# Landing the first weight tiles in idle activation tiles, and moving casts behind the q/k result

## The chip, the cores and the metric

The kernel runs on one core of a Trainium2 chip. The metric is the device time of one execution in microseconds; less is better.

## The reference

One decoder layer on 256 tokens of width 1024, in float32:

```python
z = h @ w_in[l]                                   # 1024 -> 512 (u) + 512 (q) + 512 (k) + 512 (v)
pool_out = multiscale_pool(u, w_pool, pool_scale) # trailing-window means, per-group linear
attn_out = moba_attention(q, k, v)                # 8 heads of 64; at 256 tokens plain causal attention
mix = concat([pool_out, attn_out]) @ w_out
h = layer_norm(ALPHA * h + mix)
h = layer_norm(ALPHA * h + memory_cross_attention(h, mem, w_xq, w_xkv, w_xo))   # 4 heads of 256
h = layer_norm(ALPHA * h + swiglu(h, w_gate, w_up, w_down))                     # inner width 2816
```

## The kernel before

Every large product is made from three float32r products (`three`, and the same by hand in `product_qk`): an operand is split into a high part, which ACT casts (L79 for weights, L280 for activations), and a low part, which DVE subtracts (L80, L281). So each weight tile w0, w1, ... that is loaded from HBM costs one ACT cast and one DVE subtraction before PE can use it. The order of the instructions on each engine is the order of the program text; no scheduler changes it.

`Stream` holds the list of all weight tiles in order of use. `fetch` issues loads, on SP's queue unless told otherwise; a load takes one of `RAW_BUFS` = 4 raw tiles, so the load of tile n goes out when tile n-4 has been cast and subtracted. `prepare` casts and subtracts the next tiles, running first what `before` has noted for a tile (loads of x, of the memory, of the norm weights). `get` hands a tile to a product; unless `held` is set it also prepares one more tile, up to `AHEAD` = 6 tiles past those used. With `held` and `loads` set it only issues loads. Weight tiles here are 256 KB for w0 to w5 (half a 128-row block of the q and k columns) and 512 KB from w6 on (a whole block, or half of a 1 MB piece).

The stretch that the change touches, in order:

- `keep_busy(BUSY)` gives PE 16 transposes of the identity, whose result nobody reads, while the first loads are under way. They wait for the identity that POOL makes.
- x arrives transposed in four steps (`load_xt`, into `xr`) and is split into `xT` (`split_xt`). The steps from block 4 on are noted with `before`, so their loads are issued when the cast of the weight tile of that block is due.
- `product_qk(k)` for the eight blocks k of 128 rows adds q and k, transposed, into four PSUM banks `pqk0` to `pqk3`: 24 matmuls of 256 columns per block. w0 to w10 hold its weights. In the last block `keep_qk` empties each bank into `qkT` as soon as it is complete, two on ACT (L311, L315) and two on DVE (L313, L317).
- From k = 6 on `held` and `loads` are set: no casts ahead, only loads. After the loop both are cleared.
- The `fac` factors of the pooling are made on DVE (L356, L357).
- The v product (`pv`, w11 to w14) takes two of the four banks that the q/k result has left; between its pieces stand `scores(0, 0)` and `scores(0, 1)` (masked scores, their maximum, exponentials on ACT, scaling on DVE). Then `probs_t(0)`, `probs_t(1)` transpose the probabilities into PSUM and copy them out to `sb` (one copy on DVE, one on ACT), between pieces of the u product (w15 to w18); `attend(0)` (L424) multiplies them with v into a bank `po` of the pool of four that the scores and the transposes use as well.
- w19 to w26 are for the memory's keys. `split_mem` splits the memory (`mr`, loaded in one piece of 1 MB) into `mT`. `load_x` loads the tokens `xt`, also 1 MB, right behind the load of w20.

The pool `acts` has nine tiles of 128 x 2048 float32 (tag `a8`), for `xt`, `xT`, `mT`, `xr`, `qkT`, `cT` and later tiles in turn.

Of the kernel before, what the change touches and what calls it, by code (L numbers as in the profile page):

```python
# [8 lines left out]
F32 = mybir.dt.float32  # L9
# [5 lines left out]
P = 128  # L15
# [16 lines left out]
RAW_BUFS, W_BUFS, AHEAD = 4, 8, 6  # L32
A8_BUFS = 9
PR_BUFS = 6
BUSY = 16


def r32(t):
# [3 lines left out]
class Stream:  # L42


    def __init__(self, nc, pool):
        self.nc, self.pool = nc, pool
        self.src, self.raws, self.tiles, self.notes = [], [], [], {}
        self.used, self.held, self.loads = 0, True, False

    def add(self, src, parts=2):  # L50

        n = src.shape[1] // parts
        first = len(self.src)
        self.src += [src[:, i * n:(i + 1) * n, :] for i in range(parts)]
        return range(first, len(self.src))
# [4 lines left out]
    def fetch(self, upto, queue):  # L60

        while len(self.raws) < upto:
            src = self.src[len(self.raws)]
            raw = self.pool.tile(list(src.shape), F32, tag="raw", name=f"w{len(self.raws)}r", bufs=RAW_BUFS)
            queue.dma_start(raw, src)
            self.raws.append(raw)

# [38 lines left out]
def decoder_layer(  # L106
# [3 lines left out]
    nc = tc.nc  # L110
    cp = ctx.enter_context(tc.tile_pool(name="const", bufs=1))
    wp = ctx.enter_context(tc.tile_pool(name="weights", bufs=W_BUFS))
    ap = ctx.enter_context(tc.tile_pool(name="acts", bufs=A8_BUFS))
# [5 lines left out]
    def a8(name, dt=F32):  # L119
        return ap.tile([P, KD, S], dt, tag="a8", name=name)  # L120

    def bank(name):
        return pb.tile([P, 512], F32, tag="b", name=name)
# [5 lines left out]
    ws = Stream(nc, wp)  # L129
# [5 lines left out]
    def rows(w, k0, c0, nk=2, width=D):  # L135
        return ws.add(w[k0 * P:(k0 + nk) * P, c0:c0 + width].rearrange("(k p) n -> p k n", p=P))

    c_qk = [ws.add(w_in[k * P:(k + 1) * P, 512:1536].rearrange("p (j n) -> p j n", j=2), 2 if k < 3 else 1)
            for k in range(KD)]
# [16 lines left out]
        nc.sync.dma_start(xt, x.rearrange("(t p) d -> p t d", p=P))  # L156

    xr = a8("xr")

    def load_xt(k, n=2):  # L160
        nc.sync.dma_start(xr[:, k:k + n, :], x_t[:, k:k + n, :])

    def split_xt(k, n=2):
        split(xT[0][:, k:k + n, :], xT[1][:, k:k + n, :], xr[:, k:k + n, :])
# [35 lines left out]
    ident = cp.tile([P, P], F32, name="ident")  # L200
# [78 lines left out]
    def split(h, l, ps):  # L279
        nc.scalar.copy(h, ps)  # L280
        nc.vector.tensor_sub(l, ps, r32(h))  # L281
# [17 lines left out]
    def keep_busy(n):  # L299

        ps = bank("busy")
        for _ in range(n):
            nc.tensor.transpose(ps[:, :P], ident, ident)

    qk = [accbank(f"pqk{i}").rearrange("p (f t) -> p f t", f=2) for i in range(4)]

# [12 lines left out]
    def product_qk(k):  # L319

        x_hi, x_lo = pair(xT, ALL, k)
        for j in range(2):
            hi, lo = ws.get(c_qk[k], j)
            for part in (((hi, x_hi), (hi, x_lo)), ((lo, x_hi),)):
                for i in (2 * j, 2 * j + 1):
                    for f in range(2):
                        c = 2 * (i % 2) + f
                        for n, (w, y) in enumerate(part):
                            nc.tensor.matmul(qk[i][:, f, :], w[:, c * P:(c + 1) * P], y,
                                             start=k == 0 and f == 0 and n == 0 and w is hi,  # L330
                                             stop=k == KD - 1 and w is lo, skip_group_check=True)
                    if k == KD - 1 and w is lo:
                        keep_qk(i)
            ws.done(c_qk[k], j)

    keep_busy(BUSY)
    for k in range(2, KD, 2):
        if k > 2:
            ws.before(c_qk[k][0], lambda k=k: load_xt(k))
        ws.before(c_qk[k][0], lambda k=k: split_xt(k))  # L340
    load_xt(0, 1)
    ws.fetch(1, nc.scalar)
# [1 line left out]
    load_xt(1, 1)  # L344
    ws.fetch(4, nc.sync)
    load_xt(2)
    split_xt(0, 1)
    ws.prepare(2)
    split_xt(1, 1)
    ws.held = False  # L350
    for k in range(KD):
        ws.held = ws.loads = k >= 6
        product_qk(k)
    ws.held = ws.loads = False
    for g, w in enumerate(WINDOWS):
# [450 lines left out]
```

## Time and profile before

| | |
|---|---|
| median of three timed runs | 391.63 us (390.73 to 391.84) |
| the profiled execution, whole | 393.3 us |
| its span, first to last instruction | 391.3 us |
| PE busy | 378.2 us |
| DVE busy | 246.1 us |
| ACT busy | 175.7 us |
| moved by DMA | 71.91 MB |

The profiled execution is one execution: every duration below comes from it. In the lists in order of time a row has the start and the length in us, the engine, the line of the kernel, the operation, what is written and read, and in brackets how long the engine stood idle before it and what ended that. A DMA row "SPq" is the issue on SP's queue; the landing is a separate figure. Tiles are named as in the program: w16r is the raw load of weight tile 16, w16h its high part, w16l its low part.

### The profile page before, as it was taken

To read this page: it belongs to the slowest core of one execution; us is meant where nothing else is said; L and a number is where in the kernel's file an instruction comes from. 1 tells how busy PE (TensorE), PEld (TensorE's weight loads), DVE (VectorE), ACT (ScalarE), POOL (GpSimd) and SP (SyncE) were. 2 spreads that over 40 slices of the span, in tenths; PEclk is the share of its full clock that TensorE was granted. 3 is DMA by queue.
4 is the path that set the end of the run, shared out by engine and by line. 5 is a ranking of instruction groups with operands and counts; after the bars stand their busy time and mean duration, and the time that the engine had idled before them with its cause. 6 is when DMAs were issued, how large, how long until landed. Compare 5 with 4: busy or idle time off the path is not lost.

```text
span 391.3 us, 5454 instructions
## 1 busy us (share of the span) xinstructions
PE 378.2 (97%) x2118; PEld 327.4 (84%) x2118; DVE 246.1 (63%) x340; ACT 175.7 (45%) x262; POOL 28.8 (7%) x35
## 2 busy tenths in 40 slices
PE   8998999999999999999999999999999999999982
PEld 8995879898888899998878888888888888888872
DVE  4467898776288775656887664557546456554274
ACT  5355766564332645545336553335446245344000
POOL 1000004700420000000500000000000000000000
PEclk9999999999999999999999999999999999999997
DMA  7879753845715884334507846663654964852011
GB/s 214 306 220 339 252 203 90 340 162 175 257 54 142 275 295 150 108 109 160 163 0 268 272 160 214 210 216 122 203 191 143 309 214 138 296 172 101 0 54 54
DMA packets 21689, 71.91 MB, mean 184 GB/s; under 512 B 2464, under 2 KB 3232, under 8 KB 21536
## 3 DMA queue, kind: packets, MB, share of 16 engines
q1 hardware_dynamic: 21232, 71.05, 55.0%
q10 hardware_dynamic: 432, 0.52, 0.4%
q8 instruction: 16, 0.26, 0.3%
q14 instruction: 9, 0.07, 0.1%
HBM read 70.52 MB, written 1.05 MB: 183 GB/s over the span
## 4 chain that ended last, share of the span: by engine, by line
PE 79%; DVE 7%; DMA 6%; ACT 4%; POOL 2%; issue 1%; SPq 0%; POOLq 0%; ACTq 0%; DVEq 0%
PE pg L223 10%; PE pg L221 10%; PE pg L222 10%; PE acc L221 7%; PE acc L223 7%; PE acc L222 7%; DMA w9r<-in_w_in 2%; PE pxk L221 2%; PE pxq L223 2%; PE pxq L221 2%; PE pxq L222 2%; PE pxk L222 2%; PE pxk L223 2%; PE xv L223 2%; PE xv L221 2%; PE xv L222 2%
## 5 line engine op out<-in xcount | busy, mean ns | idle before, releaser
L710 DVE TENSOR_TENSOR sg<-sg,pg 128x256 f32<-128x256 f32 x22 | 9.2, 420 | 34.9 <-ACT sg L709 34.9
L709 ACT ACTIVATE sg<-pg 128x256 f32<-128x256 f32 x22 | 8.4, 383 | 47.0 <-PE pg L223 46.8
L544 POOL TENSOR_TENSOR rs<-rs,mhalf 128x1 f32<-128x1 f32 x6 | 5.7, 955 | 199.2 <-DVE rs L543 199.2
L533 DVE SCALAR_TENSOR_TENSOR r<-h,acc 128x256 f32<-128x256 f32 (+1 forms) x12 | 6.0, 501 | 13.0 <-PE acc L223 13.0
L281 DVE TENSOR_TENSOR gTl<-pgt,gTh 128x512 fp32r<-128x512 f32 x11 | 7.1, 686 | 9.7 <-ACT gTh L280 9.7
L363 ACT ACTIVATE pr<-pr,mx 128x128 f32<-128x128 f32 (+1 forms) x16 | 7.2, 448 | 12.0 <-DVE mx L374 11.8
L280 ACT CAST gTh<-pgt 128x512 fp32r<-128x512 f32 x11 | 6.0, 589 | 14.4 <-PE pgt L716 14.4
L363 ACT ACTIVATE xpr<-xs,mx 128x256 f32<-128x256 f32 x8 | 3.7, 470 | 12.4 <-DVE mx L374 12.4
L536 DVE BATCH_NORM_STATS2 st<-r 128x6 f32<-128x512 f32 (+1 forms) x16 | 9.0, 560 | 0.5
L548 DVE SCALAR_TENSOR_TENSOR r<-r,mv,g 128x512 f32<-128x512 f32 (+1 forms) x14 | 9.2, 668 | 0.0
L436 POOL TENSOR_TENSOR win<-upad 128x271 f32<-128x271 f32 x4 | 3.6, 891 | 61.6 <-DVE pr L370 61.6
L280 ACT CAST h2Th<-tp 128x512 fp32r<-128x512 f32 x4 | 2.4, 588 | 11.8 <-PE tp L291 11.8
L80 POOL TENSOR_TENSOR w61l<-w61r,w61h 128x1024 fp32r<-128x1024 f32 x1 | 2.4, 2442 | 69.9 <-ACT w61h L79 69.9
L553 DVE SCALAR_TENSOR_TENSOR h<-r,rs,b 128x512 f32<-128x512 f32 x8 | 6.0, 752 | 1.9 <-POOL rs L544 1.8
L436 POOL TENSOR_TENSOR win<-win 128x269 f32<-128x269 f32 (+2 forms) x6 | 6.7, 1118 | 0.5
L533 DVE SCALAR_TENSOR_TENSOR r<-xt,acc 128x512 f32<-128x512 f32 x4 | 2.7, 681 | 6.0 <-PE acc L223 6.0
L716 PEld LDWEIGHTS pgt<-ident,sg 128*128 128x128 f32 x44 | 5.2, 140 | 0.8
L716 PE MATMUL pgt<-ident,sg 128*128 128x128 f32 x44 | 5.8, 272 | 0.0
L368 DVE RECIPROCAL sm<-sm 128x2 f32<-128x2 f32 x12 | 2.0, 164 | 5.9 <-ACT xpr L363 4.5
L281 DVE TENSOR_TENSOR xTl<-xr,xTh 128x512 fp32r<-128x512 f32 (+1 forms) x5 | 2.9, 582 | 4.3 <-ACT xTh L280 4.2
L374 DVE TENSOR_REDUCE mx<-xs 128x2 f32<-128x512 f32 x4 | 2.8, 692 | 4.4 <-PE xs L223 4.4
L291 PEld LDWEIGHTS tp<-ident,h 128*128 128x128 f32 x32 | 3.8, 140 | 2.0 <-issue 0.7
(1085 smaller groups left out, 1428.8 us busy)
## 6 DMA issues: line engine op xcount, KB each, us to landing
g<-in_ln_g SPq DMA_DIRECT2D x3, 512.0 KB, 7.1
b<-in_ln_b SPq DMA_DIRECT2D x3, 512.0 KB, 8.0
mr<-in_mem_t SPq DMA_DIRECT2D x1, 1024.0 KB, 7.3
xt<-in_x SPq DMA_DIRECT2D x1, 1024.0 KB, 7.8
xr<-in_x_t SPq DMA_DIRECT2D x3, 256.0 KB, 5.6
w6r<-in_w_in SPq DMA_DIRECT2D x1, 512.0 KB, 4.8
w7r<-in_w_in SPq DMA_DIRECT2D x1, 512.0 KB, 6.9
w8r<-in_w_in SPq DMA_DIRECT2D x1, 512.0 KB, 8.6
```

What stands on the lines that cost most here:

```text
L221: nc.tensor.matmul(ps, wa, ya, start=start, stop=False, skip_group_check=part)
L222: nc.tensor.matmul(ps, wa, yb, start=False, stop=False, skip_group_check=part)
L223: nc.tensor.matmul(ps, wb, ya, start=False, stop=stop, skip_group_check=part)
L280: nc.scalar.copy(h, ps)
L281: nc.vector.tensor_sub(l, ps, r32(h))
L363: nc.scalar.activation(dst[:, j, :], src[:, j, :], AF.Exp, bias=mx[:, j:j + 1], scale=1.0, accum_out=sm[:, j:j + 1])
L436: nc.gpsimd.tensor_add(nxt[:, 2 * n - 1:], cur[:, 2 * n - 1:], cur[:, n - 1:PADW + S - n])
L533: nc.vector.scalar_tensor_tensor(self.r[:, s], self.tok[:, s], ALPHA, acc, op0=OP.mult, op1=OP.add)
L536: nc.vector.bn_stats(self.st[:, self.n, :], self.r[:, c0:c1])
L548: nc.vector.scalar_tensor_tensor(self.r[:, s], self.r[:, s], self.mv[:, 0:1], gb[self.i][0][:, s], op0=OP.subtract, op1=OP.mult)
L710: nc.vector.tensor_mul(sg, sg, ps[:, CW:])
L716: nc.tensor.transpose(pt[:, f, t * P:(t + 1) * P], sgs[c][:, t, f * P:(f + 1) * P], ident)
```

## The change

The first seven weight tiles no longer take raw tiles: `homes` gives each of them a part of one of two `a8` tiles. The loads of w4 to w10 and of all of x are issued in one go before the first cast, instead of one by one as raw tiles come free and as casts fall due. From w7 on the raw tiles are used as before, so w7 to w10 have the four of them from the start and w11 waits for w7's.

`held` and `loads` are set from block 5 on instead of 6. In the built program that moves the casts of w12 and w13 from before `keep_qk` to behind it on ACT and DVE, those of w14 and w15 from before `scores(0, 0)` to behind it, and that of w16 from before `scores(0, 1)` to behind it. The order of SP's loads stays the same.

`keep_busy` gives PE nine plain products of a tile of zeros (`spark`, set by DVE), instead of sixteen transposes of the identity.

```diff
-BUSY = 16
+BUSY = 9
...
+        self.homes = {}
...
         while len(self.raws) < upto:
             src = self.src[len(self.raws)]
-            raw = self.pool.tile(list(src.shape), F32, tag="raw", name=f"w{len(self.raws)}r", bufs=RAW_BUFS)
+            raw = self.homes.pop(len(self.raws), None)
+            if raw is None:
+                raw = self.pool.tile(list(src.shape), F32, tag="raw", name=f"w{len(self.raws)}r", bufs=RAW_BUFS)
             queue.dma_start(raw, src)
...
     xr = a8("xr")
+    for i in range(2):
+        home = ap.tile([P, 4, 512], F32, tag="a8", name=f"w0to{3 + 3 * i}")
+        if i == 0:
+            ws.homes.update({n: home[:, n:n + 1, :] for n in range(4)})
+        else:
+            ws.homes.update({4: home[:, 0:1, :], 5: home[:, 1:2, :], 6: home[:, 2:4, :]})
...
         ps = bank("busy")
+        spark = cp.tile([P, P], F32, name="spark")
+        nc.vector.memset(spark, 0.0)
         for _ in range(n):
-            nc.tensor.transpose(ps[:, :P], ident, ident)
+            nc.tensor.matmul(ps[:, :P], spark, spark, start=True, stop=True)
...
     for k in range(2, KD, 2):
-        if k > 2:
-            ws.before(c_qk[k][0], lambda k=k: load_xt(k))
         ws.before(c_qk[k][0], lambda k=k: split_xt(k))
...
     ws.fetch(4, nc.sync)
     load_xt(2)
+    ws.fetch(7, nc.sync)
+    load_xt(4)
+    ws.fetch(9, nc.sync)
+    load_xt(6)
+    ws.fetch(11, nc.sync)
     split_xt(0, 1)
...
     for k in range(KD):
-        ws.held = ws.loads = k >= 6
+        ws.held = ws.loads = k >= 5
         product_qk(k)
```

## The prediction, made before the changed kernel ran

> **What bounds the kernel now.** I read the page first, then busy time by stretch, then the order of time on PE, ACT, DVE and SP around the first 60 us, then the DMA issues. The page, its first line and its chain:
>
> ```profile
> span 391.3 us, 5454 instructions
> ...
> PE 79%; DVE 7%; DMA 6%; ACT 4%; POOL 2%; issue 1%; SPq 0%; POOLq 0%; ACTq 0%; DVEq 0%
> ```
>
> PE bounds it; the chain's other 21% are waits that PE has somewhere. Busy time by stretch tells where (columns: length, then PE, PEld, DVE, ACT, POOL, granted clock, DMA share, GB/s):
>
> ```profile
> 0.00:5.00 5.00, 3.64 (x17) 3.56 (x18) 0.73 (x2) 2.21 (x3) 1.48 (x11) 1.00 0.58 144
> ...
> 30.00:40.00 10.00, 8.49 (x44) 6.26 (x45) 8.32 (x21) 6.43 (x14) 0.00 (x0) 1.00 0.97 338
> ...
> 50.00:60.00 10.00, 9.46 (x79) 8.15 (x80) 9.38 (x19) 5.01 (x13) 0.00 (x0) 1.00 0.50 171
> ...
> 100.00:200.00 100.00, 100.00 (x597) 88.76 (x596) 67.48 (x98) 42.80 (x66) 13.35 (x8) 1.00 0.50 162
> ```
>
> From 100 to 200 us PE has no gap to catch up in, so a microsecond won or lost before reaches the end whole. In 30 to 60 us DVE is nearly as full as PE. PE in order of time (start, length, work, wait in front):
>
> ```profile
> 29.15 0.64 PE L329 MATMUL pqk<-xTh,w10l 128*128 128x256 f32 x4
> 31.51 0.50 PE L221 MATMUL pv<-w11h,xTh 128*128 128x512 f32 x1 [1.71 <-ACT qkT L311]
> ...
> 45.62 0.33 PE L408 MATMUL pt<-ident,pr 128*128 128x128 f32 x1 [0.28 <-DVE pr L370]
> ...
> 51.25 0.66 PE L424 MATMUL po<-sb,vt 128*64 128x256 f32 x4 [0.45 <-ACT sb L413]
> ```
>
> The q/k product ends with four matmuls at 29.15. With single records of 0.28, (0.64-0.28)/3 = 0.12 us is the pace, so PE is free at 29.63 and waits until 31.51 for the emptying of its banks (L311). ACT shows why, and also the queue in front of the last wait, at 51.25:
>
> ```profile
> 29.91 1.04 ACT L79 CAST w13h<-w13r 128x1024 fp32r<-128x1024 f32 x1 [2.06 <-DMA w13r<-in_w_in]
> 30.86 0.59 ACT L311 ACTIVATE qkT<-pqk 128x512 f32<-128x512 f32 x1
> ...
> 44.88 1.03 ACT L79 CAST w17h<-w17r 128x1024 fp32r<-128x1024 f32 x1
> ...
> 48.93 1.06 ACT L79 CAST w20h<-w20r 128x1024 fp32r<-128x1024 f32 x1
> ```
>
> L311 stands behind the cast of w13, which waits for its load. PE's `attend(0)` at 51.25 needs a bank that the `sb` copy of `probs_t(1)` frees; that copy stands on ACT behind w20h and mTh. From the start of w20h to PE's release are 51.25-48.93 = 2.32 us.
>
> **The change, part by part.** *Earlier loads.* PE around the first 512 KB tile:
>
> ```profile
> 13.92 0.64 PE L329 MATMUL pqk<-xTh,w5l 128*128 128x256 f32 x4
> 14.71 0.39 PE L329 MATMUL pqk<-xTh,w6h 128*128 128x256 f32 x1 [0.15 <-ACT w6h L79]
> 14.94 0.28 PE L329 MATMUL pqk<-xTl,w6h 128*128 128x256 f32 x1
> ...
> 15.65 0.28 PE L329 MATMUL pqk<-xTl,w6h 128*128 128x256 f32 x1
> 15.97 0.74 PE L329 MATMUL pqk<-xTh,w6l 128*128 128x256 f32 x4
> ```
>
> Against the pace, 13.92 to 14.71 is 0.79 instead of 0.48, 14.71 to 14.94 is 0.11 over, 15.65 to 15.97 is 0.20 over: 0.62 us. With raw tiles of their own, w4 to w6 need not wait for earlier subtractions, so I take all 0.62 as gone (bounds: 0, if a longer queue slows its members, and 0.62). w0 to w3 and the first x pieces go out as before, and the order of the loads on SP stays w6, x, w7, w8, x, w9, so no x piece arrives later in the line. "At once" is eight deep: in the built program each load after the eighth waits for the landing of the one eight before it.
>
> *Fillers.* How they and the first products run:
>
> ```profile
> 0.73 0.20 POOL masks.py:197 MEMSET ident<- 128x128 f32 x1 [0.29 <-POOLq L779]
> 1.36 3.68 PE L303 MATMUL busy<-ident 128*128 128x128 f32 x16 [1.36 <-POOL ident masks.py:199]
> 4.71 0.58 PE L329 MATMUL pqk<-xTh,w0h 128*128 128x256 f32 x1
> ...
> 6.38 0.41 PE L329 MATMUL pqk<-xTl,w0h 128*128 128x256 f32 x1
> 6.59 0.78 PE L329 MATMUL pqk<-xTh,w0l 128*128 128x256 f32 x4
> ...
> 7.45 0.62 ACT L79 CAST w2h<-w2r 128x512 fp32r<-128x512 f32 x1 [0.31 <-DMA w2r<-in_w_in]
> ```
>
> and, from the instructions of one line (durations in ns: least, median, most; first and last start):
>
> ```profile
> L447 PE MATMUL pm<-upad,wpl x8: 377/378/454, 70.1 to 82.2; 128*128 128x256 f32 x8
> ```
>
> Sixteen transposes take 3.68 us, 0.23 each. A plain f32 product leaves two records (L447: 8 for 4 products), each 378-283 = 95 ns longer than a 256-column fp32r one, so 0.12+0.095 = 0.215; 128 columns take half of that, two records 0.215, and at the slow pace below about double, 0.43 us. Nine are 3.9 us. Their zeros come from one DVE memset on an idle engine; with POOL's memset (ends 0.93) as nearest row they start at about 1.0 and end at 4.9, as now (1.36+3.68 = 5.04): nothing lost. The first products are paced 6.59-4.71 = 1.88 us at 0.21 (6.38 to 6.59) instead of 0.12, though the granted clock reads 1.00 from the first stretch on. A full pace from the start saves 1.88 x (1-0.12/0.21) = 0.8 us. But then PE is through the 24 products of block 0 at 4.9+24 x 0.12 = 7.8, and w2h is ready only at 7.45+0.62 = 8.07: 0.3 of it turns into a wait. I take 0.5 won, with 0 and 0.8 as the ends; as fillers of zeros are not in the trace, nothing won stays open. The Trainium skill, "TensorE: Matmul & The Clock Gate", Part 4, says that transposes do not count as PE-busy the way products do, and Part 1 gives a window of 3.4 us; by it product fillers raise the clock sooner than transposes, and the sum comes out up to 0.3 us lower than here. This trace is half with it: the pace changes 1.9 us after the first product, sooner than transposes that count for nothing would let it.
>
> *Casts held from block 5.* On ACT and DVE the casts of w12 and w13 now stand behind the four `keep_qk`; w14 and w15 behind `scores(0,0)`; w16 behind `scores(0,1)`. The 1.88 us wait at 29.63 goes: L311 and L313 can run while PE still multiplies the k half. But DVE does the same work later, and SP's loads hang on it. DVE's rows and SP's:
>
> ```profile
> 32.73 0.68 DVE L317 COPY qkT<-pqk 128x512 f32<-128x512 f32 x1
> 33.33 0.39 DVE L356 TENSOR_SCALAR fac<-cnt 128x16 f32<-128x16 f32 x4
> ...
> 34.23 1.16 DVE L80 TENSOR_TENSOR w14l<-w14r,w14h 128x1024 fp32r<-128x1024 f32 x1
> ...
> 36.43 0.42 DVE L392 TENSOR_TENSOR pr<-ps,tri 128x256 f32<-128x256 f32 x1
> ...
> 39.98 1.23 DVE L80 TENSOR_TENSOR w16l<-w16r,w16h 128x1024 fp32r<-128x1024 f32 x1 [0.26 <-ACT w16h L79]
> 41.12 0.69 DVE L392 TENSOR_TENSOR pr<-ps,tri 128x512 f32<-128x512 f32 x1
> ...
> 45.94 1.23 DVE L80 TENSOR_TENSOR w17l<-w17r,w17h 128x1024 fp32r<-128x1024 f32 x1
> ```
>
> ```profile
> SPq L65 <- DVE w16l L80: 4.0, 1, 4.0
> ```
>
> ```profile
> 41.23 0.33 SPq L65 DMA_DIRECT2D w20r<-in_w_xk  x1
> 41.61 0.43 SPq L156 DMA_DIRECT2D xt<-in_x  x1
> ```
>
> ```profile
> w20r<-in_w_xk SPq DMA_DIRECT2D x1, 512.0 KB, 5.7
> ...
> w16r<-in_w_u SPq DMA_DIRECT2D x1, 512.0 KB, 5.3
> ...
> w25r<-in_w_xk SPq DMA_DIRECT2D x1, 512.0 KB, 3.8
> ...
> w32r<-in_w_out SPq DMA_DIRECT2D x1, 512.0 KB, 3.3
> ```
>
> The load of w20 reuses w16's raw tile, so it goes out at 41.23, when w16l ends (39.98+1.23 = 41.21), and the cast of w20 at 48.93 finds it landed at 46.9. Now w16l comes after `scores(0,1)`. The chain: q/k ends at 29.63-0.62-0.5 = 28.5, its last record at 28.66. DVE from there: L317 0.60 (32.73 to 33.33), `fac` 0.90, two casts 2.20 (34.23 to 36.43), `scores(0,0)` up to the next cast 3.55 (36.43 to 39.98), two casts 2 x 1.14, `scores(0,1)` 4.82 (41.12 to 45.94), w16l 1.23: 15.58, so 44.24, and w20 is issued at 44.26, three us later than now. ACT comes to w20h much sooner: `scores(0,1)` begins at 38.19, 3.76 later (41.12 to 44.88) come w16h, 0.95 (29.91 to 30.86), and the 4.05 from w17h to w20h: 46.95. So ACT waits for the load; queued behind it are mTh and the `sb` copy, and PE waits for that copy. If the load takes L, w20h starts at 44.26+L instead of 48.93 and `attend(0)` is L-4.67 later than now; after it the three engines' queues are the same as before. For L the rows go from 3.3 to 5.7; the nearest are its own 5.7, with xt right behind as here, and 5.3 for w16, also with 1 MB right behind. I take 5.5: +0.83 us. PE itself comes to `attend(0)` early, so a shorter wait on the way (0.28 at 45.62 now; a new one for w12l, ready only at 28.66+0.60+0.90+1.16 = 31.3) costs nothing of its own, and the 1.88 us won only lengthen the wait there. Of all gains the 1.1 us that start the chain sooner (0.62+0.5) are kept, and they are in the sum. The a8 tiles that the homes use are free by then; the built program adds no wait for them.
>
> *Sum.* The profiled execution took 393.3 us with a span of 391.3; by the sum it would take 394.1. The three timed runs have a median of 391.63, 1.7 below it, so I shift that: 392.4. Under 0.3% (1.2 us) either way is about what a measurement of this kernel can tell from no change.
>
> **Rivals.** *Faster: the load lands soon.* With nothing else under way at 44 us, w20 could land like w25 (3.8 us, after a lull) or w32 (3.3): -0.9 or -1.4 us, 390.8 or 390.3; ACT's own queue sets the floor at 46.95-48.93 = -2.0, 389.6. For it: eager loads leave the queues empty by then. Against: xt's 1 MB follows 0.4 us behind, as in the 5.7. Over 0.3% faster needs L under 3.5; chance 0.16. The Trainium skill, "DMA: Bandwidth & Descriptors", Anatomy of one DMA, fits 2.0 us plus bytes/436 GB/s (for another kind of queue): for 512 KB an estimate of 3.2 us, and by it the change would be -1.5 us, 390.2. The w20 row is 2.5 us above it, w32's 0.1.
>
> *Slower: the load lands late.* In the kernel before, w21 goes out when w17l ends, 45.94+1.23 = 47.17, six us behind w20; in the changed one w17l follows w16l at once and w21 comes 1.14 us behind w20, so three loads share the queue. If w20 then takes 6.2, the change is +1.5: 393.2. It decides from L = 5.85; chance 0.22. The same end is reached with 5.7 if the fillers save nothing (+1.5): 0.06.
>
> *The loads do not come sooner.* If the deep queue only stretches each load, the 0.62 stays and adds to +0.83: +1.45, 393.1; chance 0.06.
>
> **How the numbers follow.** The forecast, within 0.3% (L from 3.5 to 5.85), has 0.50. The three slower cases together have 0.34: 5.7 is the load's own row, and 0.15 us more decides. Faster has 0.16: it needs the shortest landings of the table in a place that now has a long one. The likeliest case gives 392.4 and reaches from 390.5 to 392.8; with the slower cases up to 393.8, the range for 8 in 10 is 390.5 to 393.8.
>
> **What would show it.** Right: no wait of PE ahead of the first `pv`, near 28.5; both `qkT` pieces ahead of w12h on ACT; w16l ending and w20r issued near 44.3; ACT waiting some 2.8 us for DMA w20r ahead of w20h; PE's longest wait ahead of `attend(0)`, released by ACT, at about 52.1. Wrong: w20r landed before ACT is there, `attend(0)` before 50 us, or a new wait of PE inside the q/k product or between 100 and 200 us.

## The result and the profile after

The changed kernel takes 396.54 us (median of four runs, 395.92 to 397.05) against 391.38 us (390.73 to 391.84) for the kernel before: ratio 1.0119, 95% interval 1.0093 to 1.0145. It is slower, where no change that can be measured was forecast, and 2.7 us beyond the upper end of the range. Its profiled execution is an ordinary one, 396.46 us with a span of 394.5. The profiled execution of before, 393.3, was not: later sessions ran that kernel 53 more times, between 390.4 and 392.44. That matters below.

The granted clock is the share of its full speed that TensorE (PE) was allowed; the page gives it in tenths, for 40 slices of the span. In the kernel after, the 6 is the slice from 49 to 59 us:

```profile
PEclk9999969999999999999999999999999999999997
```

Where PE waited (after; total us, times, longest):

```profile
PE po L438 <- ACT sb L427: 2.4, 1, 2.4
...
PE ps L401 <- DVE sb L426: 0.7, 1, 0.7
PE ps L401 <- ACT sb L427: 0.5, 1, 0.5
PE pv L231 <- DVE w12l L83: 0.3, 1, 0.3
```

The 1.7 us ahead of the first `pv` are gone. Inside the q/k product the waits at w6 are gone too, but a smaller one, which that list does not show, has come at w4h: 11.03 to 11.74 is 0.71 instead of 0.48. PE (after):

```profile
11.03 0.64 PE L340 MATMUL pqk<-xTh,w3l 128*128 128x256 f32 x4
11.74 0.38 PE L340 MATMUL pqk<-xTh,w4h 128*128 128x256 f32 x1
```

ACT, before and then after:

```profile
9.35 0.62 ACT L79 CAST w4h<-w4r 128x512 fp32r<-128x512 f32 x1
```

```profile
11.07 0.62 ACT L82 CAST w4h<-w0to 128x512 fp32r<-128x512 f32 x1 [1.43 <-DMA w0to<-in_w_in]
```

The load of w4 goes out sooner, at 3.59 instead of 5.41, and its tile is ready later. Nor did all loads go out ahead of the first weight's cast (w0h, at 4.17): those of w7 to w10 were issued at 6.38, 7.76, 9.02 and 11.07. The last is the moment at which w4's load, eight before it on SP, had landed.

Around `attend(0)` there are three new waits close together. PE in order of time (after):

```profile
29.11 0.40 PE L230 MATMUL pv<-w11h,xTh 128*128 128x512 f32 x1
...
47.77 0.48 PE L401 MATMUL ps<-qkT 64*128 64x128 f32 x2 [0.47 <-ACT sb L427]
48.96 0.71 PE L401 MATMUL ps<-qkT 64*128 64x128 f32 x6 [0.71 <-DVE sb L426]
52.12 1.13 PE L438 MATMUL po<-sb,vt 128*64 128x256 f32 x4 [2.44 <-ACT sb L427]
53.03 0.65 PE L439 MATMUL po<-sb,vt 128*64 128x128 f32 x4
53.60 0.58 PE L230 MATMUL pu<-xTh,w15h 128*128 128x256 f32 x1
53.98 0.42 PE L231 MATMUL pu<-xTl,w15h 128*128 128x256 f32 x1
54.20 0.41 PE L232 MATMUL pu<-xTh,w15l 128*128 128x256 f32 x1
...
57.40 0.41 PE L232 MATMUL pu<-xTh,w16l 128*128 128x256 f32 x1
...
59.85 0.28 PE L231 MATMUL pu<-xTl,w16h 128*128 128x256 f32 x1
```

From 52.12 to about 57.5 PE runs at little more than half pace: single products are 0.41 long and 0.21 apart, instead of 0.28 and 0.12. The stretches of the same kernel (length, PE busy, granted clock, DMA share, GB/s) date it as well:

```profile
45.00:50.00 5.00, 3.49 (x28) 1.00 0.72 246
50.00:55.00 5.00, 2.88 (x14) 0.60 0.99 387
55.00:60.00 5.00, 5.00 (x33) 0.72 0.27 107
60.00:65.00 5.00, 5.00 (x44) 1.00 0.35 105
```

What holds PE back is the chain that was forecast. DVE:

```profile
38.85 0.68 DVE L406 TENSOR_TENSOR pr<-ps,tri 128x512 f32<-128x512 f32 x1
...
43.68 1.23 DVE L83 TENSOR_TENSOR w16l<-w16r,w16h 128x1024 fp32r<-128x1024 f32 x1
```

SP and then ACT:

```profile
44.93 0.33 SPq L68 DMA_DIRECT2D w20r<-in_w_xk  x1
```

```profile
47.35 0.37 ACT L427 COPY sb<-pt 128x256 f32<-128x256 f32 x1
49.80 1.04 ACT L82 CAST w20h<-w20r 128x1024 fp32r<-128x1024 f32 x1 [2.08 <-DMA w20r<-in_w_xk]
50.75 1.04 ACT L289 CAST mTh<-mr 128x1024 fp32r<-128x1024 f32 x1
51.70 0.36 ACT L427 COPY sb<-pt 128x256 f32<-128x256 f32 x1
```

w16l comes behind `scores(0, 1)`, w20's load goes out behind w16l, ACT stands 2.08 us at w20h, and behind it stands the copy for which `attend(0)` waits.

**One subtraction orders the runs.** Take the time of each profiled execution and subtract the start of its `attend(0)`, the first `po` row:

| profiled execution | us | `attend(0)` at | rest |
|---|---|---|---|
| before | 393.3 | 51.25 | 342.05 |
| before with the new fillers | 392.1 | 50.06 | 342.04 |
| after, held from block 6 | 390.34 | 48.31 | 342.03 |
| before with the loads edit | 389.59 | 47.55 | 342.04 |
| after with the wait filled | 394.49 | 52.46 | 342.03 |
| before, held from block 5 | 395.31 | 52.09 | 343.22 |
| after with the old fillers | 395.72 | 51.90 | 343.82 |
| after | 396.46 | 52.12 | 344.34 |

Where no slow records (products at the slow pace) follow `attend(0)`, the rest is 342.04 within 0.02; runs 8 and 10 below give 342.05 and 342.06. Where they follow, it is 1.2 to 2.3 longer. Two more profiles below have other rests: run 6 with 343.32 (slow records) and run 9 with 342.58 (a wait of 0.5 further on, ahead of `pm`). So but for run 9's wait a run's time is the start of `attend(0)`, plus 342.04, plus what half pace costs. For after the last term is 2.30; 18 slow products at 0.21 - 0.12 = 0.09 and the 0.67 by which its first `po` group is longer than that of before (1.48 from 52.12 to 53.60, against 0.81) make 2.3 as well. The same subtraction puts `attend(0)` of an ordinary execution of before, 391.6, at about 49.6, an estimate: the profiled one, at 51.25, was late by 1.7. Of the 4.9 us between 396.5 and 391.6, then, about 2.5 are a later `attend(0)` and 2.3 the half pace behind it.

### The profile page after: what moved, and what is told of

Same layout as the page of the kernel before. It is cut to its first block, busy times and chain, and to the rows that moved or that the text cites. A ratio compares the mean times of both kernels' runs of the same rounds, so it can differ in the third digit from the quotient of the medians.

```text
span 394.5 us, 5454 instructions
## 1 busy us (share of the span) xinstructions
PE 380.4 (96%) x2120; PEld 329.5 (84%) x2120; DVE 246.6 (63%) x341; ACT 175.9 (45%) x262; POOL 28.6 (7%) x35
## 3 DMA queue, kind: packets, MB, share of 16 engines
HBM read 70.52 MB, written 1.05 MB: 181 GB/s over the span
## 4 chain that ended last, share of the span: by engine, by line
PE 83%; DVE 7%; DMA 3%; ACT 2%; issue 2%; POOL 2%; SPq 1%; POOLq 0%; ACTq 0%; DVEq 0%
PE pg L232 10%; PE pg L231 10%; PE pg L230 10%; PE acc L230 7%; PE acc L231 7%; PE acc L232 7%; PE pqk L340 4%; PE pxk L230 2%; PE pxq L230 2%; PE pxq L232 2%; PE pxq L231 2%; PE pxk L231 2%; PE pxk L232 2%; DMA w0to<-in_w_in 2%; PE xv L232 2%; PE xv L230 2%
## 5 line engine op out<-in xcount | busy, mean ns | idle before, releaser
L450 POOL TENSOR_TENSOR win<-win 128x269 f32<-128x269 f32 (+2 forms) x6 | 5.7, 958 | 0.5
L438 PE MATMUL po<-sb,vt 128*64 128x256 f32 x16 | 3.1, 469 | 2.4 <-ACT sb L427 2.4
```

Source lines behind the costliest of these rows:

```text
L450: nc.gpsimd.tensor_add(nxt[:, 2 * n - 1:], cur[:, 2 * n - 1:], cur[:, n - 1:PADW + S - n])
```

## The experiments

Theory A: holding the casts from block 5 makes the late chain; its waits push PE to half pace; loads and fillers do no harm. Rival B: the eight-deep loads cost. Rival C: the fillers of zeros cost. Rivals D and E question the two halves of A. Each run was compared with runs of the kernel before on the same chip.

**1. After, held from block 6 again.**

```diff
-        ws.held = ws.loads = k >= 5
+        ws.held = ws.loads = k >= 6
```

> The changed kernel, but casts are held from block 6 again (loads and fillers stay changed). Theory A (the casts held from block 5 push w16l, and behind it w20's load, to 44.9 us; ScalarE then stands at w20h in front of the copy that attend(0) needs, TensorE waits 0.47 + 0.71 + 2.44 us and falls to about half pace until 57.5): the 2.44 us wait ahead of attend(0) is gone or under 0.7, the 128x256 records after it stay at 0.28, and the median is back near the kernel before, 391 to 392. Rival B (the early loads into the activation tiles cost, by slower landings): the median stays above 394. Rival C (the fillers of zeros cost): the median stays near 393.3, two above the kernel before.

Measured: 390.04 us (five runs, 389.75 to 390.58) against 391.72, ratio 0.9961 (0.9947 to 0.9974). PE:

```profile
48.31 0.66 PE L438 MATMUL po<-sb,vt 128*64 128x256 f32 x4 [0.45 <-ACT sb L427]
```

DVE:

```profile
37.03 1.22 DVE L83 TENSOR_TENSOR w16l<-w16r,w16h 128x1024 fp32r<-128x1024 f32 x1 [0.26 <-ACT w16h L82]
```

One number undoes the whole loss and more: w16l starts 6.65 us earlier than in after. B and C fall as causes of the loss, as loads and fillers are still the changed ones. It is also faster than the kernel before, by more than A expected.

**2. Before, held from block 5.** The same line, in the kernel before, from 6 to 5.

> The kernel before with one edit: casts are held from block 5 instead of block 6. Theory A: the holding alone delays w16l and w20's load; TensorE's wait ahead of attend(0) grows from 0.45 to 1.5 us or more, slow records follow it, and the median is 394 to 396.5. Rival B or C (the loads or the fillers cost): the median stays within 0.7 of the kernel before (391.4), as the loads and fillers are untouched.

Measured: 396.16 us (four runs, 395.31 to 397.02) against 391.72, ratio 1.0116 (1.0091 to 1.014): the whole loss, without the other two edits. PE's waits:

```profile
PE po L424 <- ACT sb L413: 2.5, 1, 2.5
...
PE ps L387 <- DVE sb L412: 0.7, 1, 0.7
PE ps L387 <- ACT sb L413: 0.5, 1, 0.5
```

PE in order of time:

```profile
29.06 0.40 PE L221 MATMUL pv<-w11h,xTh 128*128 128x512 f32 x1
...
52.09 1.13 PE L424 MATMUL po<-sb,vt 128*64 128x256 f32 x4 [2.48 <-ACT sb L413]
```

It starts the first `pv` at 29.06 and `attend(0)` at 52.09, both within 0.05 of after. With the casts held from block 5, the earlier loads bring nothing that these runs can tell from nothing.

**3 and 4. The fillers: after with the 16 transposes, before with the nine products of zeros.** The edits are the diff's hunks of `keep_busy` and `BUSY`, taken back and made alone.

> The changed kernel, but with the 16 transposes of the identity ahead of the first product again. Theory A: no change from the changed kernel, 396.0 to 397.0. Rival C (the fillers of zeros bring full pace later than the transposes in most executions, about 1.9 us, the distance of the kernel before's profiled execution from its timed runs): the median falls to about 394.6, and the first full-pace record comes earlier than 6.6 us.

> The kernel before with one edit: nine products of zeros in place of the 16 transposes as fillers. Theory A: within 0.7 of the kernel before (391.4). Rival C: about 1.9 slower, 393.3. If the product counts for TensorE's pace and the transpose does not (the Trainium skill, "TensorE: Matmul & The Clock Gate", says so of transposes): up to 0.8 faster, full pace before 5.5 us.

Measured: 395.46 us (four runs, 395.17 to 397.03) for the third, whose runs overlap those of after; 391.82 (ten runs, 390.92 to 392.36) for the fourth, ratio 1.0004 (0.9993 to 1.0015). Fillers do nothing that can be measured on the kernel before, so C falls. On after the 1.1 us between the medians stay unclear: the profiles differ by 0.74 us, 0.22 of it at `attend(0)` and 0.52 in the length of the slow stretch, which varies from run to run. When full pace comes up differs between executions with either kind. Products of zeros, early (run 1):

```profile
4.76 0.28 PE L340 MATMUL pqk<-xTl,w0h 128*128 128x256 f32 x1
```

and late (after):

```profile
6.55 0.32 PE L340 MATMUL pqk<-xTl,w0h 128*128 128x256 f32 x1
```

Transposes, early (run 3):

```profile
5.24 0.28 PE L338 MATMUL pqk<-xTh,w0h 128*128 128x256 f32 x1
```

and late (run 2):

```profile
7.39 0.30 PE L329 MATMUL pqk<-xTh,w1h 128*128 128x256 f32 x1
```

Run 4 is the kernel before in all but the fillers, and its `pv` row tells how an ordinary execution of that kernel differs from the profiled one, 1.2 us earlier with a shorter wait:

```profile
30.30 0.50 PE L221 MATMUL pv<-w11h,xTh 128*128 128x512 f32 x1 [1.17 <-ACT qkT L313]
```

**5. After, with the wait filled.** Ten products of zeros behind `scores(1, 0)`, into an unused quarter of its bank:

```diff
+FILL = 10
...
+    sparks = []
...
+        sparks.append(spark)
...
+        if (hq, t) == (1, 0):
+            for _ in range(FILL):
+                nc.tensor.matmul(pss[1][:, 1, P:], sparks[0], sparks[0], start=True, stop=True)
```

> The changed kernel plus ten products of zeros right behind scores(1, 0), into the unused quarter of its bank, so that TensorE works through most of its 2.44 us wait ahead of attend(0); the wait's cause is left as it is. Theory A in two parts (the wait itself costs 0.9 us against the kernel before, the half pace after it 2.5): attend(0) still starts near 52.1, the 128x256 records after it are 0.28 in place of 0.41, and the median falls by about 2.4 to 394.1 (393.6 to 394.7). Rival D (the pace falls for another reason, and the idle time has nothing to do with it): records after attend(0) stay at 0.41 and the median stays at 396 to 397.

Measured: 394.86 us (four runs, 394.49 to 395.92) against 391.57, ratio 1.0093 (1.007 to 1.0116); 1.7 below after, where 2.4 were expected. The median is 0.16 above the upper end of the expected range. PE:

```profile
49.21 0.71 PE L405 MATMUL ps<-qkT 64*128 64x128 f32 x6 [0.67 <-DVE sb L433]
49.85 2.50 PE L409 MATMUL ps<-spark 128*128 128x128 f32 x20
52.46 0.66 PE L445 MATMUL po<-sb,vt 128*64 128x256 f32 x4
52.94 0.40 PE L446 MATMUL po<-sb,vt 128*64 128x128 f32 x4
53.27 0.39 PE L231 MATMUL pu<-xTh,w15h 128*128 128x256 f32 x1
```

The wait's cause is untouched, `attend(0)` comes no sooner (52.46), and no slow record follows; the granted clock is 1.00 throughout and the rest is 342.03. So it is the idle time that costs the pace, and D falls. The DMA share from 50 to 55 us is 0.99 in run 5 as in after, so the traffic alone does not slow PE. The fall is smaller than expected in part because `attend(0)` came 0.34 later; and some of after's runs may lose less than the profiled one's 2.30 to half pace (395.92 - 52.12 - 342.04 = 1.76 for the fastest, if its `attend(0)` was there too).

**6. After, with w20 prepared one step later.**

```diff
+    ws.held = True
     run(u, 4)
+    ws.held = False
     split_mem(0)
     probs_t(1)
```

> The changed kernel, casts still held from block 5, but w20 is prepared one step later, so that on ScalarE the copy of probs_t(1) stands ahead of w20h and no longer behind its load. Theory A: the wait ahead of attend(0) falls from 2.44 to below 0.7, no slow records follow, and the median is 391.5 to 393, though w16l and w20's load are as late as in the changed kernel (w20r issued near 44.9). Rival E (the late chain on VectorE itself holds TensorE, ScalarE's place in the queue does not matter): the wait only changes its name (to the copies on VectorE) and the median stays above 395.

Measured: 392.37 us (ten runs, 391.75 to 393.81) against 391.57, ratio 1.0027 (1.0013 to 1.0041). ACT:

```profile
48.51 1.07 ACT L289 CAST mTh<-mr 128x1024 fp32r<-128x1024 f32 x1
49.46 0.39 ACT L427 COPY sb<-pt 128x256 f32<-128x256 f32 x1
50.37 1.05 ACT L82 CAST w20h<-w20r 128x1024 fp32r<-128x1024 f32 x1 [0.52 <-DMA w20r<-in_w_xk]
```

w20h still waits for its load, but the copy no longer stands behind it, and 4.2 of the 4.9 us are back. So it is ACT's order that turned a late load into a stall, and E falls. One thing went otherwise: the 2.44 wait is gone, yet slow records followed in the profiled execution, at 393.81 the slowest of the ten (in run 9, with waits of 0.45 and 0.72, none did):

```profile
48.69 0.48 PE L401 MATMUL ps<-qkT 64*128 64x128 f32 x2 [0.51 <-ACT sb L427]
49.85 0.71 PE L401 MATMUL ps<-qkT 64*128 64x128 f32 x6 [0.68 <-DVE sb L426]
50.49 0.66 PE L438 MATMUL po<-sb,vt 128*64 128x256 f32 x4
50.97 0.57 PE L439 MATMUL po<-sb,vt 128*64 128x128 f32 x4
51.48 0.58 PE L230 MATMUL pu<-xTh,w15h 128*128 128x256 f32 x1
51.86 0.41 PE L231 MATMUL pu<-xTl,w15h 128*128 128x256 f32 x1
```

**7, 8 and 10. The loads edit alone; after held from block 7; the loads edit held from block 7.** The loads edit is `homes`, the three new `fetch` and two new `load_xt` calls, and the notes of `load_xt` taken out.

> The kernel before with the loads edit alone (old fillers, casts held from block 6). If the gain of the changed kernel with casts held from block 6 (0.9961 of the kernel before) comes from the loads: 389.7 to 390.4. If it needs the new fillers as well: 391 to 392.

> The changed kernel with casts held from block 7 only, so that w14 is cast ahead of the q/k copies and w16 ahead of scores(0, 0). Theory A (what counts is where w16l stands on VectorE, since it frees w20's tile): w20r is issued at least 2 us earlier than with block 6 (38.3), attend(0) doesn't wait, and the median is 389.4 to 390.4; if the cast of w14 stands in front of the q/k copies while its load is late, a wait ahead of the first pv product comes back and the median is 390.5 to 391.5.

> The kernel before with the loads edit and casts held from block 7, old fillers: the two settings that each gave about 389.9, together. If the moment of w16l no longer decides anything once attend(0) doesn't wait: 389.4 to 390.2, the same as the loads alone. If each had its own gain: 388.3 to 389.2.

Measured: 389.88 (five runs, 389.41 to 389.98), ratio 0.9957 (0.9942 to 0.9972); 389.9 (ten runs, 388.69 to 391.53), ratio 0.9963 (0.9947 to 0.9979); 389.81 (ten runs, 388.94 to 391.05), ratio 0.9958 (0.9944 to 0.9972). The loads alone gain 1.7 us, and neither the fillers nor block 7 add to it. In run 8 a small wait ahead of the first `pv` came back, 0.29, behind the cast of w14; its median did not rise with it. PE of run 7, with old fillers and casts held from block 6:

```profile
28.80 0.40 PE L230 MATMUL pv<-w11h,xTh 128*128 128x512 f32 x1
...
47.55 0.66 PE L436 MATMUL po<-sb,vt 128*64 128x256 f32 x4 [0.44 <-ACT sb L425]
```

and ACT of the same run:

```profile
24.73 1.05 ACT L82 CAST w13h<-w13r 128x1024 fp32r<-128x1024 f32 x1 [0.23 <-DMA w13r<-in_w_in]
```

The wait ahead of the first `pv` (1.71 in before, 1.17 in run 4) is gone here too: the cast of w13 starts at 24.73 instead of 29.91 (28.71 in run 4) and is long done when the banks are to be emptied. That is where the loads gain: the q/k product itself ends at 28.80, hardly sooner than run 4's 28.97 (its last four matmuls at 28.49, plus 0.48). And the time is passed on, since w16l stays ahead of `scores(0, 1)`. In run 8 w16l starts at 33.19 and `attend(0)` at 47.66, hardly sooner than run 1's 48.31: once w20 is there in time, w16l's place decides nothing more.

**9. Before, held from block 5, w20 prepared one step later.** The edit of run 6 on the kernel of run 2.

> The kernel before with casts held from block 5, and w20 prepared one step later as in the run that moved the copy of probs_t(1) ahead of w20h; loads and fillers are those of before. Theory A: the 4.4 us that the holding alone cost are mostly gone, 391.7 to 393.3, attend(0) waits under 0.7 us. Rival E (the late chain on VectorE costs by itself): 395 or more.

Measured: 392.23 us (ten runs, 391.99 to 393.21) against 391.52, ratio 1.0027 (1.0015 to 1.004). Two lines of order take back 3.9 of run 2's 4.4 us, with none of the other edits in it.

## Why the prediction was wrong, point by point

- **Earlier loads, 0.62 us.** The waits at w6 went, as forecast, but a new one came inside the product, which the prediction lists as a sign of being wrong. ACT waited 1.43 us for w4's load and cast it 1.7 us later than before; PE lost at least 0.23 there in after, and stood idle 0.85 there in run 1 and 0.83 in run 6. Taking "all 0.62 as gone" was the upper bound; the lower one, that a longer queue slows its members, came true for w4. The gain did not reach the first `pv`: 29.06 without the loads edit (run 2), 29.11 with it. With casts held from block 5 its worth was nothing that can be told, with block 6 it was 1.7 us.
- **Fillers, 0.5 us.** Not found: 0.1 slower with an interval across 1 (run 4). The start and end of the fillers were right in after (1.05 to about 4.9). What was wrong is that the kind of filler sets when full pace comes. It came between 4.8 and 7.4 us, early and late with either kind (runs 1, 2, 3 and after, above). By the Trainium skill, "TensorE: Matmul & The Clock Gate", Part 4, products should have been sooner; the runs do not bear that out. The Trainium skill says in Part 1 of the same page that the activity window runs freely and does not start with the kernel; a moment that shifts by some 2.5 us between executions agrees with that, though by more than the half microsecond that the Trainium skill names there.
- **The 1.88 us wait goes, and only lengthens the later one.** Right for the kernel as changed. In run 7 the same wait is gone and the time is kept.
- **The chain to w20h.** The path was right, and the best part: w16l ends at 44.91 (forecast 44.24), w20r is issued at 44.93 (44.26), its landing took 4.5 us (5.5 was taken, from rows of 3.3 to 5.7), w20h starts at 49.80 (49.76), `attend(0)` at 52.12 (52.08). That the last two agree within 0.04 is luck: q/k ended 0.6 late, so the load went out 0.67 late; it landed 1.0 sooner, and by these figures the cast started 0.37 behind the landing. PE's longest wait stands where it was announced, with ACT's copy as its releaser.
- **What followed from the wait: the failed step.** "PE itself comes to `attend(0)` early", and its waiting there was priced at the lateness of `attend(0)` alone, +0.83. The three waits, 0.47, 0.71 and 2.44 us, also cost the pace of the next 5.4 us, 2.30 in the profiled execution. Nothing in the sum or in the rivals stood for that, although the prediction itself priced half pace at the start.
- **The base: the second failed step.** "The three timed runs have a median of 391.63, 1.7 below it, so I shift that". The start of `attend(0)` after the change was worked out in absolute time, from the chain, and came true within 0.04. That it would be 1.7 sooner in ordinary executions was assumed, and the runs speak against it: with block 5 held and w20 prepared early, four profiled executions (after and runs 2, 3 and 5) have it at 51.90 to 52.46, none near 50.4. Run 4 shows part of the reason: of the 1.2 us by which it is ahead of the profiled execution of before at the first `pv`, 0.54 lie in the wait there (1.17 against 1.71), which the change removes anyway. Against the profiled execution of before, `attend(0)` of after is 0.87 late; against an ordinary one, with `attend(0)` at the estimated 49.6, it is 2.5 late. Subtracting 1.7 from the sum took away time that the changed kernel does spend.
- **Rivals.** The slower one named a late landing (5.85 and more, for xt and w21 close behind); w20 landed in 4.5, so the sign came with another mechanism. The one that the loads do not come sooner was right for w4, but does not explain the loss: run 7, with the same loads, is faster than before. The faster one needed less than 3.5; the row is 1.0 above that, with the DMA share at 0.72 and 0.99 from 45 to 55 us. The Trainium skill ("DMA: Bandwidth & Descriptors", Anatomy of one DMA) has a fit for another kind of queue that gives an estimate of 3.2 us; the row is 1.3 above it.

With the two steps mended, 52.08 + 342.04 + 2.30 = 396.4, against 396.54 measured; the 2.30 is known only from after, and the 52.08 is right by luck.

## What to carry to other kernels

When an edit moves work behind other work on one engine, follow it through every queue up to the wait at which the bounding engine stands, and price that wait twice: its length, and the pace that PE loses behind it. Where a chain gives a point in absolute time, compare it with that point in ordinary executions of the kernel before, not with the one profiled execution, and don't shift both by the same amount. And a late load costs only what stands behind its first user: moving one copy ahead of the cast that waits gave back most of the loss.

## What the runs showed of the hardware

- Half pace came after idle times shorter than expected: 0.47, 0.71 and 2.44 us within five in after, and once after 0.51 and 0.68 alone (run 6), but not after 0.45 and 0.72 (run 9). A single wait of 0.45 (run 1) did not bring it, nor did one of 1.71 (before). The Trainium skill ("TensorE: Matmul & The Clock Gate", HAM oscillation) gives idle gaps of more than about 3.4 us as the limit; no single gap here is that long, so the runs do not agree with it as a safe limit. What sum of gaps, over what window, decides is open: it was not measured by itself.
- Loads issued sooner, with more of them under way, can be there later: the cast of w4 started at 10.74 to 11.94 in the eight profiled executions with the loads edit and at 9.26 to 9.35 in the four without, while that of w7 came sooner (14.87 in after, 16.62 in before).
- Ten products of zeros, whose result nobody reads, held the pace through the wait (granted clock 1.00 in run 5, 0.60 and 0.72 in after).
- At the start of the kernel products are slow while the granted clock reads 1.00; at 50 to 60 us it reads 0.60 and 0.72. The clock column alone shows only one of these two slow stretches; the length of single records shows both.
